# A trunk step on one core: the opening rebuilt around the first half of the tokens

## The chip, the cores and the metric

The kernel runs on one core of one Trainium2 chip, in one launch. The metric is the device time of an execution in microseconds (us); a profile beside it shows what each engine did. Engines are named as the profile names them: PE (TensorE matmuls), PEld (its weight loads), DVE (VectorE), ACT (ScalarE), POOL (GpSimd), SP (the engine that issues most DMAs).

## What is computed

One layer of a hybrid trunk over 640 tokens (512 latent, 128 context) of width 1024, in fp32. The change touches the first of its three blocks alone, the SwiGLU feed-forward with adaLN modulation:

```python
mods = (silu(cvec) @ w_ada + b_ada).reshape(9, 1024)     # one row of cvec for latent, one for context tokens
hh = rmsnorm(x, g_norm[0]) * (1 + m[1]) + m[0]
x = x + 0.5 * m[2] * ((silu(hh @ ffn1_w1) * (hh @ ffn1_w3)) @ ffn1_w2)
...
```

Behind it stand the token mixer (differential attention beside a two-way mLSTM) and a second block of this form. `ffn1_w1` and `ffn1_w3` are 1024 x 2816.

## The kernel before

Activations lie transposed: 128 partitions of features, eight pieces `d` (or `k`) of 128 features, and 640 tokens along the free axis. The tokens are cut into two halves of 320 (`HALF`); the second holds 192 latent and all 128 context tokens, which take other modulations, so a piece of it is handled in two segments of 192 and 128 (`SEGS`). A fp32 product is made of three matmuls on rounded operands (`mm3`, line 133): each operand is split into a high part (an ACT copy into `fp32r`) and a low part (DVE subtracts the high part), and high times high, high times low and low times high are added up. So every weight and every activation costs an ACT and a DVE instruction before PE can use it.

The hidden width is cut into 11 blocks of 256. Block 0 is multiplied plainly (`HalfStep.plain`, line 313) in the opening; blocks 1 to 10 go through `products` (line 406) as granules, w1 and w3 of a block in turn, with a scheme of seven products that replaces eight. That scheme needs sums and differences of the activations (`operand_sums`, line 330: a hand-ordered chain of 16 DVE instructions of 640 elements and their ACT copies) and of the weights (`Granule.parts`, line 245, which splits two pieces into wB and wC and forms sums in place in `raw`, and `Granule.sums`, line 263, which splits the 2048 columns of `raw` into ww). A granule's weights have two buffers of each kind, and `raw` has two.

The opening (lines 92 to 820) goes like this. SP loads the conditioning vectors, both halves of x, small constants, and then, in turn, eight pieces `raw_a` of 1 MB of the adaLN weights and the weights of block 0. `Modulate.__init__` squares x on ACT and adds on DVE (`Stats`, line 165), for both halves; PE adds over partitions by a matmul with ones (`ps_ss`), and ACT and DVE make the reciprocal root (`rstd_of`, line 154). `weights` splits block 0's w1 and w3 in halves; the low part of w1 is subtracted on POOL, that of w3 on DVE. Then the loop over `k`: `product(k)` is the adaLN product (16 small matmuls, `ps_a`), a DVE copy brings it to `small`, `columns(k)` turns it to columns with four tiny matmuls (`ps_at`), DVE makes `mod` and `scale`, and `norm` (line 764) makes both halves of piece k: for each segment DVE scales by scale and rstd, ACT adds the shift into the high part, DVE subtracts. After that `plain` uses piece k for three units (f, half) out of four, 18 matmuls; in each step the columns of piece k+1 and the product of k+2 stand ahead of the matmuls of k (`before`, line 772). The fourth unit, 48 matmuls, comes behind the loop. `shifts` then adds the shift to x itself on ACT, and `operand_sums` starts. The first granule's parts and sums are made as soon as their operands and an engine allow.

What sets the order: matmuls stay in the order of the program, and so do SP's transfers up to the load of `ident`. ACT, DVE and POOL are ordered by a planner of the compiler, by its own estimates and by place in the program; `issue_after(ins)` queues instructions behind `ins` on its engine.

Of the kernel before, what the change touches and what calls it, by code (L numbers as in the profile page):

```python
# [31 lines left out]
def tile_trunk(ctx: ExitStack, tc: tile.TileContext, a: dict):  # L32
# [61 lines left out]
    for hf in range(2):  # L94
        dma(x_all[:, :, hf * HALF : (hf + 1) * HALF], a["x"][:, :, hf * HALF : (hf + 1) * HALF])
    sel = load(cp, [128, 2], a["sel"], name="sel")
    b_ada = load(cp, [128, 72], a["b_ada"], name="b_ada")
    g_norm = load(cp, [128, 3, KT], a["g_norm"], name="g_norm")
# [196 lines left out]
    class HalfStep:  # L295
# [110 lines left out]
        def products(self, work, between, then=(), behind=None, prepared=False):  # L406
# [8 lines left out]
            if not prepared:  # L415
                work[0][0].parts(self.fp)
                work[0][0].sums()
# [97 lines left out]
        def run_whole(self, x, gate, final, between):  # L515
# [13 lines left out]
            self.products(work, between, down[:2])  # L529
# [163 lines left out]
    with ExitStack() as ph:  # L693
# [11 lines left out]
        class Modulate:  # L705


            def __init__(self):
                self.raw, self.row = {}, {}
                self.rs = []  # L710
                x = [x_all[:, d, :] for d in range(KT)]
                st = [Stats(x, hf, ntmp) for hf in range(2)]
                for hf in range(2):
                    for d in range(KT):
                        st[hf].add(d)
                    self.rs.append(st[hf].rstd(psum))
                self.load(0)

            def weights(self, w1, w3):

                W = [[wp.tile([128, 2048], F32R, tag="w" + t, name="wH") for t in "HL"] for _ in range(2)]
                raws = [rawp.tile([128, 2048], F32, tag="raw", name="raw") for _ in range(2)]
                for k in range(2):
                    cs = slice(1024 * k, 1024 * k + 1024)
                    for raw, src, (h, lo), eng in zip(raws, (w1, w3), W, (pool_e, vec)):
                        dma(raw[:, cs], src[:, 4 * k : 4 * k + 4])
                        act(h[:, cs], raw[:, cs], AF.Copy)
                        tt(eng, lo[:, cs], raw[:, cs], h[:, cs].bitcast(F32), ALU.subtract)
                    self.load(k + 1)
                self.load(3)  # L730
                return W
# [21 lines left out]
            def columns(self, k):  # L753
# [7 lines left out]
                for hf in range(2):  # L761
                    self.norm(hf, k)

            def norm(self, hf, d):

                c0 = hf * HALF
                S = hs.hh(d, hf)
                for s0, s1, j in SEGS[hf]:
                    xs = x_all[:, d, s0:s1]
                    h, lo = (t[:, s0 - c0 : s1 - c0] for t in S)  # L770
                    sh = m_of(0)[:, d, j : j + 1]
                    stt(xs, xs, scale[:, 0, d, j : j + 1], self.rs[hf][:, s0 - c0 : s1 - c0], ALU.mult, ALU.mult)
                    act(h, xs, AF.Identity, bias=sh)
                    stt(lo, xs, sh, h.bitcast(F32), ALU.add, ALU.subtract)

            def before(self, k):
                if k == 0:
                    self.product(0)
                    self.columns(0)
                    self.product(1)  # L780
                    self.columns(1)
                    self.product(2)
                elif k + 1 < KT:
                    self.columns(k + 1)
                    if k + 2 < KT:
                        self.product(k + 2)

            def shifts(self):
                for d in range(KT):
                    for s0, s1, j in ((0, NS, 0), (NS, T, 1)):  # L790
                        xs = x_all[:, d, s0:s1]
                        act(xs, xs, AF.Identity, bias=m_of(0)[:, d, j : j + 1])

        psum.order = [6, 7]
        start = Modulate()
        W = start.weights(a["w1a"][0], a["w3a"][0])
        units = [(0, 0), (1, 0), (0, 1)]
        psum.order = list(range(6))
        ps = {u: [acc_tile(psum) for _ in range(2)] for u in units}
# [8 lines left out]
        for u in units:  # L808
            hs.gate_plain(*u, ps[u])
        for i in range(2):  # L810
            hs.up[i].load()
        psum.order = [6, 7, 0, 1, 2, 3, 4, 5]
        ps = [acc_tile(psum) for _ in range(2)]
# [88 lines left out]
        hs.run_whole(resid, half_m[:, 0], to_mixing, modulation)  # L902
# [1101 lines left out]
```

## Time and profile before

| what | value |
|---|---|
| median of 3 runs | 1873.93 us (1870.94 to 1876.59) |
| the profiled execution | 1874.16 us |
| its span in the profile | 1872.4 us |
| PE, DVE, ACT, POOL busy | 97%, 69%, 45%, 2% of the span |
| mean granted TensorE clock | 0.988 |

Times of the trace are counted from the start of the span. Rows of the chain of waits give start, length and what ran; rows of the instructions in order of time add the engine, the line, the tiles written and read, and the count; rows of groups give count, busy time, mean length of one in ns, and idle time ahead of them. Stretches give busy time and count of PE, PEld, DVE, ACT and POOL, the granted clock as a share of full speed, the share of the DMA engines' time and GB/s. Most DVE rows carry line 39 or 42, those of the helpers `tt` and `stt`; they are told apart by their tiles.

### The profile page before, as it was taken

The page shows a single profiled execution, that of the slowest core. Times are in us where ns is not written, and L with a number is a line of the kernel's source. Part 1 is how long each engine was busy: PE and PEld are TensorE (multiplying, and loading weights), DVE is VectorE, ACT ScalarE, POOL GpSimd, SP SyncE. Part 2 cuts the span into 40 slices and gives each one's busy share as a digit, 9 for nine tenths or more (in the row PEclk, how much of TensorE's full clock was granted, in tenths as well). Part 3 has the DMA queues.
Part 4 walks back from the last instruction along what each step waited for, and adds up shares of the span by engine and source line. Part 5 has one row for each costly group of instructions (what it writes and reads, how often), then busy time and mean ns, then how long its engine had stood idle before and what let it go on. Part 6 is the DMA issues. An engine that isn't in the chain of part 4 may idle for free.

```text
span 1872.4 us, 30753 instructions
## 1 busy us (share of the span) xinstructions
PE 1812.7 (97%) x12658; PEld 1774.4 (95%) x12658; DVE 1300.2 (69%) x2177; ACT 849.6 (45%) x1455; POOL 35.8 (2%) x57
## 2 busy tenths in 40 slices
PE   5899999999999999999999989999999999999999
PEld 4899999999998999999999979999999899999999
DVE  6888886576786675865755537875456778887585
ACT  5644444112554353453454436565235645554232
POOL 1000001110000000000000000000000000000000
PEclk8899999999999999999999999999999999999999
DMA  8344547964324322322222254566442344457972
GB/s 328 119 142 168 192 169 260 382 213 146 118 81 133 123 74 95 120 77 95 98 79 83 74 178 128 187 208 218 167 134 95 130 140 153 171 177 250 336 275 91
DMA packets 127293, 299.81 MB, mean 160 GB/s; under 512 B 9457, under 2 KB 90609, under 8 KB 114353
## 3 DMA queue, kind: packets, MB, share of 16 engines
q1 hardware_dynamic: 117890, 257.49, 40.0%
q0 software_dynamic: 9264, 40.37, 5.9%
q8 instruction: 99, 1.62, 0.4%
q14 instruction: 40, 0.33, 0.0%
HBM read 234.20 MB, written 63.63 MB: 159 GB/s over the span
## 4 chain that ended last, share of the span: by engine, by line
PE 86%; DVE 7%; DMA 4%; ACT 2%; issue 1%; SPq 0%; DVEq 0%; ACTq 0%
PE ps_f L52 41%; PE ps_p L52 22%; PE ps_t L52 12%; PE ps_o L52 2%; PE sc L52 2%; PE ps_n L52 2%; PE ps_u L52 1%; DMA ada<-csil_dram 1%; PE ps_wT L55 1%; DVE ww L39 1%; PE ps_qkT L55 1%; DMA P<-nm_dram 1%; DMA so<-o_dram 0%; DVE wL L39 0%; DMA raw_a<-in_w_ada_c 0%
## 5 line engine op out<-in xcount | busy, mean ns | idle before, releaser
L52 PE MATMUL ps_f<-S,ww 128*128 128x320 f32 x1992 | 322.9, 311 | 6.7 <-ACT ww L267 4.2
L52 PEld LDWEIGHTS ps_f<-S,ww 128*128 128x128 f32 x1992 | 301.1, 189 | 9.7 <-ACT ww L267 4.5
L52 PE MATMUL ps_p<-hH,wH 128*128 128x320 f32 x864 | 274.0, 317 | 3.1 <-ACT aT L1325 2.5
L52 PE MATMUL ps_p<-hH,wL 128*128 128x320 f32 x864 | 267.3, 309 | 0.0
L52 PE MATMUL ps_p<-hL,wH 128*128 128x320 f32 x864 | 267.2, 309 | 0.0
L52 PE MATMUL ps_f<-hm,ww 128*128 128x320 f32 x1248 | 198.2, 311 | 2.0 <-DVE ww L39 2.0
L52 PEld LDWEIGHTS ps_f<-hm,ww 128*128 128x128 f32 x1248 | 188.2, 190 | 2.3 <-DVE ww L39 2.2
L52 PE MATMUL ps_t<-wH,hH 128*128 128x256 f32 x640 | 185.7, 290 | 1.0 <-DVE x L42 1.0
L52 PE MATMUL ps_t<-wH,hL 128*128 128x256 f32 x640 | 181.8, 284 | 0.0
L52 PE MATMUL ps_t<-wL,hH 128*128 128x256 f32 x640 | 181.5, 284 | 0.0
L52 PEld LDWEIGHTS ps_p<-hH,wH 128*128 128x128 f32 x864 | 162.8, 188 | 4.4 <-ACT aT L1325 2.7
L39 DVE TENSOR_TENSOR ww<-raw,ww 128x2048 fp32r<-128x2048 f32 (+1 forms) x62 | 138.7, 2237 | 37.7 <-ACT ww L267 18.7
L52 PEld LDWEIGHTS ps_p<-hL,wH 128*128 128x128 f32 x864 | 162.8, 188 | 0.5
L52 PEld LDWEIGHTS ps_p<-hH,wL 128*128 128x128 f32 x864 | 162.5, 188 | 0.0
L52 PE MATMUL ps_f<-hm,wB 128*128 128x320 f32 x1008 | 161.5, 309 | 0.0
L52 PEld LDWEIGHTS ps_f<-hm,wB 128*128 128x128 f32 x1008 | 151.3, 188 | 0.0
L39 DVE TENSOR_TENSOR wL<-raw,wH 128x2048 fp32r<-128x2048 f32 x49 | 112.1, 2289 | 38.2 <-ACT wH L123 38.1
L123 ACT ACTIVATE wH<-raw 128x2048 fp32r<-128x2048 f32 x49 | 93.6, 1911 | 89.4 <-PE ps_p L52 85.5
L39 DVE TENSOR_TENSOR raw<-raw 128x1024 f32<-128x1024 f32 x144 | 124.6, 865 | 1.9
L52 PEld LDWEIGHTS ps_t<-wH,hH 128*128 128x128 f32 x640 | 123.1, 192 | 2.0 <-issue 1.2
L52 PEld LDWEIGHTS ps_t<-wH,hL 128*128 128x128 f32 x640 | 123.1, 192 | 0.5 <-DVE hL L42 0.5
L52 PEld LDWEIGHTS ps_t<-wL,hH 128*128 128x128 f32 x640 | 123.3, 193 | 0.2
(295 smaller groups left out, 3206.0 us busy)
## 6 DMA issues: line engine op xcount, KB each, us to landing
g_dram<-g SPq DMA_DIRECT2D x44, 640.0 KB, 5.1
raw_a<-in_w_ada_c SPq DMA_DIRECT2D x24, 512.0 KB, 4.0
raw<-in_w1b SPq DMA_DIRECT2D x11, 1024.0 KB, 4.9
raw<-in_w3b SPq DMA_DIRECT2D x11, 1024.0 KB, 4.8
raw<-in_w1a SPq DMA_DIRECT2D x10, 1024.0 KB, 4.8
raw<-in_w3a SPq DMA_DIRECT2D x10, 1024.0 KB, 6.4
ada<-in_w_ada_c POOLq DMA_DIRECT2D x18, 512.0 KB, 5.3
hm<-g_dram POOLq DMA_DIRECT2D x7, 1280.0 KB, 9.6
```

Source lines behind the costliest of these rows:

```text
L39: return eng.tensor_tensor(out=out, in0=in0, in1=in1, op=op)
L52: tc.keep_in_program_order(nc.tensor.matmul(*args, **kw))
L55: tc.keep_in_program_order(nc.tensor.transpose(*args, **kw))
L123: act(h, raw, AF.Copy)
```

## The change

1. Transfers: of x only the first half is loaded at the start, in two pieces of four `d`; the second half comes behind two more `raw_a`, and block 0's weights and the small constants are moved too.
2. The first loop runs over half 0 alone: four units (two f, w1 and w3), 12 matmuls a step. The two units of half 1 for both weights, 96 matmuls, come behind it. In each step the product of k+1 stands ahead of the matmuls of k and the columns of k+1 behind them.
3. The norm: DVE multiplies whole pieces by rstd (`scaled`), ACT applies scale and shift twice, into the high part and into x (`norm`), and DVE subtracts (`low`). For half 1 (`second`), pieces 2, 3, 6 and 7 get scale and shift on DVE by tensor_scalar and one ACT copy for two pieces. `shifts` goes.
4. The second half's statistics, its rstd and the later half of block 0's weight splits move into the loop (steps 1, 3, 5 and 2), queued behind the norm of that step.
5. All subtractions of block 0's weights are DVE's.
6. The first granule's parts are queued behind the first two pieces of half 1 (`first`), the second granule's parts on DVE behind the S2 part of the operand sums (`behind`), where they had been behind the first granule's split.

```diff
     cT = load(cp, [128, KT, 2], a["cT"], name="cT")
-    for hf in range(2):
-        dma(x_all[:, :, hf * HALF : (hf + 1) * HALF], a["x"][:, :, hf * HALF : (hf + 1) * HALF])
...
+    for k in range(0, KT, 4):
+        dma(x_all[:, k : k + 4, :HALF], a["x"][:, k : k + 4, :HALF])
...
-        def products(self, work, between, then=(), behind=None, prepared=False):
+        def products(self, work, between, then=(), behind=None, prepared=False, first=()):
...
-                work[0][0].parts(self.fp)
+                with ExitStack() as st:
+                    for ins in first:
+                        st.enter_context(tc.issue_after(ins))
+                    work[0][0].parts(self.fp)
                 work[0][0].sums()
...
-            self.products(work, between, down[:2])
+            self.products(work, between, down[:2], behind=behind, first=first)
...
+                self.add(0, 0, KT)
                 self.load(0)
+                for t, n in ((sel, "sel"), (b_ada, "b_ada"), (g_norm, "g_norm")):
+                    dma(t, a[n])
+                self.raws = raws
+                self.fetch((w1, w3), 0)
+                self.load(1)
+                self.load(2)
+                dma(x_all[:, :, half(1)], a["x"][:, :, half(1)])
+                self.load(3)
+                self.fetch((w1, w3), 1)
+                self.weights(0)
+                self.rstd(0)
...
+            def weights(self, k):
+                cs = slice(1024 * k, 1024 * k + 1024)
+                for raw, (h, lo) in zip(self.raws, self.W):
+                    act(h[:, cs], raw[:, cs], AF.Copy)
+                    tt(vec, lo[:, cs], raw[:, cs], h[:, cs].bitcast(F32), ALU.subtract)
...
                 scale_of(0, 1, k, k + 1)
-                for hf in range(2):
-                    self.norm(hf, k)
+                if k == 0:
+                    self.scaled(0, 0, 1)
+                self.norm(0, k)
+                if k == 0:
+                    self.scaled(0, 1, 4)
+                self.low(0, k, 1)
+                if k == 0:
+                    self.scaled(0, 4, KT)
+
+            def scaled(self, hf, d0, d1):
+                xs = x_all[:, d0:d1, half(hf)]
+                tt(vec, xs, xs, self.rs[hf][:, None, :].to_broadcast([128, d1 - d0, HALF]), ALU.mult)
 
             def norm(self, hf, d):
...
-                    stt(xs, xs, scale[:, 0, d, j : j + 1], self.rs[hf][:, s0 - c0 : s1 - c0], ALU.mult, ALU.mult)
-                    act(h, xs, AF.Identity, bias=sh)
-                    stt(lo, xs, sh, h.bitcast(F32), ALU.add, ALU.subtract)
...
+                    by = dict(scale=scale[:, 0, d, j : j + 1], bias=m_of(0)[:, d, j : j + 1])
+                    act(h[:, s0 - c0 : s1 - c0], xs, AF.Identity, **by)
+                    self.at_act = act(xs, xs, AF.Identity, **by).ins
+
+            def low(self, hf, d, n):
+                p, k = hs.part[d // 4, hf], slice(d % 4, d % 4 + n)
+                self.at_vec = tt(vec, p[:, 1, k], x_all[:, d : d + n, half(hf)], p[:, 0, k].bitcast(F32), ALU.subtract).ins
+
+            def second(self, d):
+                if d % 4:
+                    self.norm_by_vec(d)
+                else:
+                    for i in (d, d + 1):
+                        self.norm(1, i)
+                self.low(1, d, 2)
+
+            def norm_by_vec(self, d):
+
+                for i in (d, d + 1):
+                    for s0, s1, j in SEGS[1]:
+                        xs = x_all[:, i, s0:s1]
+                        ts(xs, xs, scale[:, 0, i, j : j + 1], ALU.mult, m_of(0)[:, i, j : j + 1], ALU.add)
+                act(hs.part[d // 4, 1][:, 0, d % 4 : d % 4 + 2], x_all[:, d : d + 2, half(1)], AF.Copy)
 
-            def before(self, k):
+            def products(self, k):
+
                 if k == 0:
                     self.product(0)
                     self.columns(0)
+                elif k + 1 < KT:
+                    self.product(k + 1)
+                yield
+                if k == 0:
                     self.product(1)
...
+                if k + 1 < KT:
+                    self.columns(k + 1)
+                with tc.issue_after(self.at_act), tc.issue_after(self.at_vec):
+                    if k in (1, 3):
+                        self.add(1, 2 * k - 2, 2 * k + 2)
+                    elif k == 2:
+                        self.weights(1)
+                if k == 5:
+                    self.rstd(1)
+                    self.scaled(1, 0, 4)
+                    self.scaled(1, 4, KT)
+                elif k > 5:
+                    self.second(2 * k - 12)
...
         for k in range(KT):
-            start.before(k)
-            for u in units:
-                for i in range(2):
-                    hs.plain(ps[u][i], W[i], *u, k)
-        vec.tensor_copy(identr, ident)
+            around = start.products(k)
+            next(around)
+            for (f, i), p in ps.items():
+                hs.plain(p, W[i], f, 0, k)
+            next(around, None)
+            if k + 2 == KT:
+                first = start.at_act, start.at_vec
+        start.second(4)
+        start.second(6)
...
         for i in range(2):
-            for k in range(KT):
-                hs.plain(ps[i], W[i], 1, 1, k)
-        hs.gate_plain(1, 1, ps)
-        start.shifts()
-        hs.operand_sums(lambda r: x_all[:, 2 * r : 2 * r + 2, :])
+            for f in range(2):
+                for k in range(KT):
+                    hs.plain(ps[f, i], W[i], f, 1, k)
+        for f in range(2):
+            hs.gate_plain(f, 1, (ps[f, 0], ps[f, 1]))
+        summed = hs.operand_sums(lambda r: x_all[:, 2 * r : 2 * r + 2, :])
```

More of the change, by code (lines that the diff above doesn't have):

```diff
@@ L513, in up_work, with run_whole @@
             ]
-        def run_whole(self, x, gate, final, between):
+        def run_whole(self, x, gate, final, between, behind, first):
             work = self.up_work()
@@ L719, in weights @@
[L719 to L729, printed above, removed]
-                self.load(3)
-                return W
+                self.st = [Stats(x, hf, ntmp) for hf in range(2)]
@@ new lines, in __init__, with add, rstd, fetch @@
+                dma(x_all[:, :, half(1)], a["x"][:, :, half(1)])
+                self.load(3)
+                self.fetch((w1, w3), 1)
+                self.weights(0)
+                self.rstd(0)
+            def add(self, hf, d0, d1):
+                for d in range(d0, d1):
+                    self.st[hf].add(d)
+            def rstd(self, hf):
+                self.rs[hf] = self.st[hf].rstd(psum)
+            def fetch(self, srcs, k):
+                for raw, src in zip(self.raws, srcs):
+                    dma(raw[:, 1024 * k : 1024 * k + 1024], src[:, 4 * k : 4 * k + 4])
@@ L800, in tile_trunk @@
+                if k == 5:
[4 more added lines that the diff above has]
+                    self.second(2 * k - 12)
+        psum.order = [6, 7]
+        start = Modulate(a["w1a"][0], a["w3a"][0])
+        W = start.W
+        psum.order = list(range(4))
+        ps = {(f, i): acc_tile(psum) for f in range(2) for i in range(2)}
         psum.order = [6, 7]
         for k in range(KT):
-            start.before(k)
```

49 lines of the change are left out of this document (15 added, 34 removed).

## The prediction

> **What bounds the kernel now.** I read the page first, then the stretches of 20 us, then the chain of waits, then the instructions in order of time from 0 to 90 us. The page says that TensorE (PE) is busy for 97% of the span, so there is little to win anywhere; the stretches say that the little is in the first 100 us.
>
> ```profile
> span 1872.4 us, 30753 instructions
> PE 1812.7 (97%) x12658; PEld 1774.4 (95%) x12658; DVE 1300.2 (69%) x2177; ACT 849.6 (45%) x1455; POOL 35.8 (2%) x57
> ```
>
> In the stretches the columns are PE, weight load, DVE, ACT, POOL, then the granted clock and the DMA. PE is full from 100 us on. Before that it lacks time in the first 30 us and in 80 to 100, and DVE is nearly full from 40 to 80.
>
> ```profile
> 20.00:40.00 20.00, 15.04 (x120) 11.44 (x116) 15.43 (x37) 9.37 (x19) 2.65 (x2) 0.74 1.02 419
> 40.00:60.00 20.00, 20.00 (x174) 17.78 (x167) 18.19 (x49) 14.76 (x30) 0.00 (x0) 1.00 0.07 27
> 60.00:80.00 20.00, 19.77 (x132) 19.05 (x130) 18.60 (x24) 13.37 (x21) 0.00 (x0) 1.00 0.25 86
> 80.00:100.00 20.00, 14.36 (x76) 13.91 (x76) 13.59 (x15) 9.55 (x11) 1.25 (x2) 0.74 0.64 224
> 100.00:120.00 20.00, 20.00 (x138) 20.00 (x137) 15.50 (x21) 8.69 (x14) 0.53 (x1) 1.00 0.49 164
> ```
>
> The chain (start, length, what) names the two places. The first loop starts at 30.3 behind the load of x, the norm and the first adaLN columns; each later turn is PE alone, 2.83 + 0.34 + 1.00 = 4.17 us. At 81.7 DVE ends the sums on the raw weights of the second granule, ACT and DVE split them in turn, and from 86.60 PE runs on for 394 matmuls. I call 86.60 the mark: behind it the work is the same in both kernels and PE is full, so the change is worth what it moves the mark.
>
> ```profile
> 1.20 6.79 DMA x<-in_x
> ...
> 12.41 2.52 PE ps_ss L52 x4
> ...
> 30.30 4.76 PE ps_f L52 x18
> ...
> 36.40 2.83 PE ps_f L52 x18
> 39.23 0.34 PE ps_at L52 x4
> 39.58 1.00 PE ps_a L52 x16
> ...
> 81.68 0.61 DVE raw L39
> 82.31 1.92 ACT ww L267
> 84.25 2.30 DVE ww L39
> ...
> 86.60 60.73 PE ps_f L52 x394
> ```
>
> **The start, up to the first matmuls.** Three things shorten it. Only half of x is needed, in two pieces: the first lands between 4.6 (half of 6.79, from 1.20) and 7.99; I take 6.2. The adds run without a gap at 0.58 us each, the first 0.88 us behind the landing; six then end at 10.6 and not at 12.36. The second half's statistics leave the start. And the GpSimd subtraction goes, which stretches DVE instructions beside it: in the same newton step one instruction takes 0.49 us and the next, under POOL's, 2.65. Twice that is 4.3 us saved.
>
> ```profile
> 8.87 3.48 DVE L39 TENSOR_TENSOR nacc<-nacc,nsq 128x320 f32<-128x320 f32 x6 [7.59 <-ACT nsq L181]
> ...
> 17.26 0.49 DVE L39 TENSOR_TENSOR rt<-rt,rv 128x320 f32<-128x320 f32 x1
> ...
> 17.73 2.35 POOL L39 TENSOR_TENSOR wH<-raw,wH 128x1024 fp32r<-128x1024 f32 x1 [17.28 <-ACT wH L727]
> 17.78 2.65 DVE L42 SCALAR_TENSOR_TENSOR ry<-rt,ry 128x320 f32<-128x320 f32 x1
> ```
>
> New start: 10.6, ps_ss 2.5, then rstd in six instructions of about 0.5 (3.1 with hand-overs) = 16.2. The two weight splits that now are both DVE's (1.2 us each, the wB row below) stand ahead of it; 1.5 us of them is not covered by ps_ss: 17.7. Then the first scaled piece 0.5, ACT's two pieces 1.05, the subtraction 0.5, and the two larger scaled pieces, which come first in the program and of which 1.2 us isn't covered by ACT: 21.0. So the loop starts fed at 21 (19 to 23) and not at 30.3.
>
> **The first loop.** A turn holds 12 matmuls for 18, so 1.89 + 0.34 + 1.00 = 3.2 us of PE. But the columns of step k+1 now stand behind the matmuls of step k, and between them and their own matmuls PE has only one product (1.00 us). In that time must pass: mod and scale 0.16 each, ACT's h and x (0.56 each, overlapping by 0.09), the subtraction 0.49, and five hand-overs of 0.04.
>
> ```profile
> L39 DVE TENSOR_TENSOR mod<-ps_at,b_ada 128x4 f32<-128x4 f32 x8 | 1.3, 158 | 4.8 <-PE ps_at L52 4.8
> L773 ACT ACTIVATE hm<-x,mod 128x320 fp32r<-128x320 f32 x8 | 4.5, 563 | 12.3 <-DVE x L42 12.2
> L746 DVE COPY small<-ps_a 128x256 f32<-128x256 f32 x8 | 3.3, 416 | 0.0
> L39 DVE TENSOR_TENSOR s<-ps_f,u 128x320 f32<-128x320 f32 x1 | 0.5, 486 | 0.0
> ```
>
> That is 2.04 us against 1.00, less one matmul that needs h alone: PE, which keeps program order and so holds all that is behind, waits 0.9 us a turn, and the turn is 4.1 us, nearly that of before for two thirds of the work. Before, the columns stood a whole step ahead and this chain was hidden. This is the step I hold to be the weak one. From 21: step 0 at half clock (12/18 of 4.76 = 3.2), product 1.0, its copy and columns 0.9, the chain 2.0 = 28.1; six turns = 52.7. What the change queues in the loop adds to it: rstd of the second half (four ps_ss on PE, 2.5 us at the start's slow pace, some 1.4 here, 0.5 beyond the wait), two weight splits on DVE (0.7 of their 2.4 reach the chain), and the scaled pieces of the second half (1280 elements each, by the g row's 1.49 us for as many), which stand ahead of mod 7 on DVE or behind it: 0 to 2.8, I take 1.8. The last step's matmuls start at 55.7 (53 to 58). DMA does not set this: before, it moved 419 GB/s in 20 to 40 us and was all but done then (27 GB/s in 40 to 60), and the loop is over no earlier here. The next granules' loads now wait for the second weight splits, near 40 us, and land about 5 us later, ahead of their use.
>
> ```profile
> raw<-in_w1a SPq DMA_DIRECT2D x10, 1024.0 KB, 4.8
> ```
>
> ```profile
> 56.19 12.56 PE L52 MATMUL ps_f<-hm,wH 128*128 128x320 f32 x84
> ```
>
> PE then has 12 + 96 matmuls, at this row's 0.15 each 16.1 us: it is done at 71.8 at the earliest, as the 96 may wait for the second half's pieces. Before, this row ended the same work at 68.7. PE is 3 us late there, but that isn't yet the mark.
>
> **DVE behind the loop.** From 61.3 to 82.3 DVE had no gap of note: these are most of its rows there (count, busy, mean ns), and the stretch is 21.0 us.
>
> ```profile
> L39 DVE TENSOR_TENSOR x<-x 128x640 f32<-128x640 f32 x7 | 5.6, 819 | 0.0
> L39 DVE TENSOR_TENSOR S<-x,S 128x640 fp32r<-128x640 f32 x6 | 4.7, 818 | 0.0
> L39 DVE TENSOR_TENSOR ww<-raw,ww 128x2048 fp32r<-128x2048 f32 x1 | 2.3, 2286 | 0.0
> L39 DVE TENSOR_TENSOR g<-SO,g 128x1280 fp32r<-128x1280 f32 x1 | 1.5, 1486 | 0.0
> L39 DVE TENSOR_TENSOR raw<-raw 128x512 f32<-128x512 f32 x2 | 1.4, 686 | 0.0
> L39 DVE TENSOR_TENSOR raw<-raw 128x1024 f32<-128x1024 f32 x1 | 1.2, 1222 | 0.0
> L39 DVE TENSOR_TENSOR wB<-raw,wB 128x1024 fp32r<-128x1024 f32 x1 | 1.2, 1218 | 0.0
> L39 DVE TENSOR_TENSOR wC<-raw,wC 128x512 fp32r<-128x512 f32 x1 | 0.7, 684 | 0.0
> ```
>
> All of it stays. What the loop did before now falls behind it: the first granule's parts (wB, wC and three raw: 4.1 us without overlaps), which the change holds back until the second half has begun; four subtractions of 640 (0.73 each when queued, 2.9); one operand sum (0.7); and eight tensor_scalar of 192 and 128. For these no row stands: above, 0.41 and 0.35 us of the fused form of the same sizes; below, 0.15; 1.2 to 3.0 in all, I take 2.0.
>
> ```profile
> L42 DVE SCALAR_TENSOR_TENSOR x<-x,scale,ry 128x192 f32<-128x192 f32 x8 | 3.3, 411 | 0.0
> L42 DVE SCALAR_TENSOR_TENSOR x<-x,scale,ry 128x128 f32<-128x128 f32 x8 | 2.8, 345 | 0.0
> ```
>
> By the Trainium skill (VectorE: DVE Perf Modes, the perf-mode tier table) an fp32 tensor_scalar in SBUF runs at twice the rate of a two-tensor form, which by its figure of 1227 ns for 2048 makes some 1.4 of these 2.0, and the mark 0.6 earlier; no row here shows it.
>
> So 21.0 + 4.1 + 2.9 + 0.7 + 2.0 = 30.7 us from 55.7, plus some 0.8 in which DVE waits for ACT, which has 18 pieces of the second half to do: 87.2 where it was 82.3, 5 us late. ACT's and DVE's last split follow as before. Dearer may be the order.
>
> ```profile
> 70.04 1.22 DVE L39 TENSOR_TENSOR wB<-raw,wB 128x1024 fp32r<-128x1024 f32 x1
> ```
>
> The first granule's parts come after the operand sums in the program. If they are done after them, its five products wait too, and up to 60 matmuls (8.9 us) are left when the second granule's weights are ready; if they are slotted in early, nothing. I take 3, nearer to early, since the row shows the second granule's wB done at 70.0, amid the sums. The mark moves by 5 + 3 = 8 us. The half clock behind the stall stays, as the stall does.
>
> **Sum.** The profiled execution took 1874.16 us around its span of 1872.4, 0.2 above the median of 1873.93. With 8 us: 1882.
>
> **Rivals.** *Faster:* the chain is hidden, turns are PE's own 3.2 us. Last step at 46.6, DVE's 30.7 end at 77.3, the mark at 81.5; with pieces of the second half done in the loop's gaps 78.5, so 1866. It decides for turns under 3.5 us. For it speaks that DVE has work for only some 23 of the loop's 35 us (1.25 a step, adds 3.5, splits 2.4, rstd 2, scaled pieces 5.4); against it, the chain, each link of which waits for the one before. *Even:* the last step at 53, the first granule's parts early: 53 + 30.7 = 83.7 for 82.3, no surcharge: 1874 to 1878. *Half clock in the loop:* PE idles a fifth of each turn. Before, it was halved behind the stall (first row, 0.50); but a stretch as thin as this loop kept it whole (second row, 1.00).
>
> ```profile
> 82.30:92.60 10.30, 6.90 (x24) 6.51 (x25) 6.55 (x6) 3.82 (x2) 0.54 (x1) 0.50 0.87 308
> 713.80:717.20 3.40, 1.92 (x15) 1.61 (x14) 3.40 (x6) 0.60 (x1) 0.00 (x0) 1.00 0.29 77
> ```
>
> If it comes, 12 matmuls cost 1.3 us more in seven turns, 9 us: 1891. The Trainium skill (TensorE: Matmul & The Clock Gate, "A second HAM failure mode: psum-queue depth-cycling") says that short idles between groups of matmuls make the clock swing; the row at 713.80 speaks against it here. *It doesn't do what it says:* a planner orders ACT and DVE, and puts splits or statistics ahead of the first norm, so that the loop starts no earlier than 27: 6 us more, 1888.
>
> **Chances.** Forecast 0.44 (its own range 1877 to 1888), even 0.20, faster 0.21, half clock 0.08, late start 0.07. A measurement of this kernel tells 0.3%, 5.6 us, from no change. Faster by more: most of its case, 0.19. Within: the even case, the lower end of the forecast and the rest, 0.26. Slower: 0.55. The range reaches down to the faster case's 1866, of which half may fall below, and up to the half clock's 1891.
>
> **What would show it.** Right: first loop matmuls near 21; turns of 4.1 with PE waiting for the subtraction of x; the last step near 55.7; DVE without gaps from there to about 87; the split of the second granule's ww behind 90. Wrong: turns of 3.2; a loop over before 50; or the first granule's parts done inside the loop. If PE never stops from the loop into the second granule, the forecast is wrong as a whole.

## The result, and the profile after

The changed kernel takes 1882.27 us (median of 4 runs, 1881.32 to 1883.22), the kernel before, run beside it, 1872.43 us: a ratio of 1.0049, 95% interval 1.0033 to 1.0065. It is slower, and 1882 was forecast. The number came out, in good part by luck: two of the steps that make it up did not come out, and one of those decides what one would repair. The profiled execution took 1883.22 us around a span of 1881.5. One execution of f2, a kernel of the experiments below, took 8873 us and is left out of its ratio.

The stretches of 20 us after, from 40 us on (columns as before: PE, weight load, DVE, ACT, POOL, granted clock, DMA):

```profile
40.00:60.00 20.00, 15.34 (x132) 11.38 (x124) 12.12 (x27) 9.85 (x17) 0.00 (x0) 1.00 0.32 121
60.00:80.00 20.00, 7.78 (x38) 7.43 (x39) 18.09 (x33) 17.32 (x33) 0.00 (x0) 0.66 0.00 0
80.00:100.00 20.00, 20.00 (x139) 20.00 (x138) 18.16 (x21) 12.42 (x15) 1.21 (x2) 1.00 0.50 157
```

Before, PE lacked 5.6 us in 80 to 100 and was full from 40 to 80. Now it is full from 80 on, but has a quarter of its time idle in 40 to 60 and 12 us in 60 to 80, where ACT and DVE are nearly full.

From 120 us on both kernels do the same work, so the simplest measure of the opening is how many matmuls PE has begun by then. One row for each kernel, before first (PE's busy time, count):

```profile
0.00:120.00 120.00, 95.18 (x643) 0.91 0.56 207
```

```profile
0.00:120.00 120.00, 83.36 (x563) 0.89 0.50 183
```

That is 80 matmuls fewer. At the pace of a full stretch (138 in 20 us, the kernel before from 100 to 120: 0.145 us each) the opening lost 11.6 us; the busy times say the same, 11.8 us. I use this count below. It is that of one execution, and good to some 2 us: three of the kernels below are the same up to the loop and start it at 25.87, 26.87 and 27.14.

Where PE stands still shows in its instructions in order of time around the last step of the first loop (start, length, count, and in brackets the idle time before and what ended it):

```profile
47.21 1.88 PE L52 MATMUL ps_f<-hm,wH 128*128 128x320 f32 x11 [0.80 <-DVE hm L39]
...
51.77 1.88 PE L52 MATMUL ps_f<-hm,wH 128*128 128x320 f32 x11 [0.80 <-DVE hm L39]
...
58.06 0.50 PE L52 MATMUL ps_at<-sel,small 128*128 128x2 f32 x4
69.50 0.64 PE L52 MATMUL ps_f<-hm,wH 128*128 128x320 f32 x1 [10.94 <-ACT hm L798]
72.85 3.57 PE L52 MATMUL ps_f<-hm,wH 128*128 128x320 f32 x12 [2.72 <-DVE hm L39]
```

The columns of the last piece are there at 58.06, yet its matmuls wait for ACT until 69.50 and for DVE until 72.85. From there PE runs on without a stop. DVE's and ACT's instructions in that time show what stood ahead:

```profile
58.33 2.89 DVE L39 TENSOR_TENSOR x<-x,ry 128x1280 f32<-128x1280 f32 x2
61.14 0.15 DVE L39 TENSOR_TENSOR mod<-ps_at,b_ada 128x4 f32<-128x4 f32 x1
61.21 1.72 DVE L48 TENSOR_SCALAR x<-x,scale,mod 128x192 f32<-128x192 f32 x6
62.84 0.15 DVE L42 SCALAR_TENSOR_TENSOR scale<-mod,g_norm 128x2 f32<-128x2 f32 x1
```

```profile
59.85 1.75 ACT L798 ACTIVATE hm<-x,mod,scale 128x192 fp32r<-128x192 f32 x4 [3.14 <-DVE x L39]
...
66.27 1.04 ACT L252 ACTIVATE wB<-raw 128x1024 fp32r<-128x1024 f32 x1
...
68.80 0.64 ACT L798 ACTIVATE hm<-x,mod,scale 128x320 fp32r<-128x320 f32 x1
```

The second half's scaled pieces stand ahead of the last piece's `mod`, six tensor_scalar of the second half ahead of its `scale`, and the second half's pieces and the copies of both granules' weights ahead of its norm on ACT.

### The profile page after: what moved, and what is told of

Its sections match the earlier page's. It is cut to its first block, busy times and chain, and to the rows that moved or that the text cites. A ratio compares the mean times of both kernels' runs of the same rounds, so it can differ in the third digit from the quotient of the medians.

```text
span 1881.5 us, 30716 instructions
## 1 busy us (share of the span) xinstructions
PE 1813.2 (96%) x12658; PEld 1774.0 (94%) x12658; DVE 1296.6 (69%) x2156; ACT 848.9 (45%) x1449; POOL 30.9 (2%) x55
## 4 chain that ended last, share of the span: by engine, by line
PE 83%; DVE 8%; DMA 4%; ACT 3%; issue 1%; SPq 0%; DVEq 0%; ACTq 0%
PE ps_f L52 38%; PE ps_p L52 22%; PE ps_t L52 12%; PE sc L52 2%; PE ps_o L52 2%; PE ps_n L52 2%; DMA ada<-csil_dram 2%; DVE ww L39 1%; PE ps_wT L55 1%; PE ps_qkT L55 1%; PE ps_u L52 1%; DMA raw<-in_w2b 1%; DVE x L39 1%; DVE hm L39 0%; DMA raw_a<-in_w_ada_c 0%
```

## The experiments

Four theories. **C**: the chain in each turn, the step that the prediction held to be the weak one. **Q**: the queue just shown, the last piece behind second-half work. **H**: behind a loop over one half, PE has nothing to do until the other half's pieces are there. **D**: VectorE's list behind the loop sets the end, as the prediction reckoned the mark. No kernel below leaves out or changes what is computed. Each ratio is to executions of the kernel before that were taken beside it, with medians of 1871.6 to 1872.5 us. The count is that of the profiled execution alone, which took 1869.8 us in e3 (median 1874.58) and 1878.47 in f2 (median 1871.1): count and median need not agree.

| kernel | us, median | ratio to before, 95% interval | matmuls by 120 us | opening against before |
|---|---|---|---|---|
| before | 1872.4 | | 643 | |
| changed | 1882.27 | 1.0049 (1.0033 to 1.0065) | 563 | -11.6 us |
| e1 last piece first | 1885.8 | 1.0069 (1.0052 to 1.0087) | 565 | -11.3 |
| e2 second half early | 1890.44 | 1.0102 (1.0087 to 1.0117) | 535 | -15.7 |
| e3 columns ahead | 1874.58 | 1.0008 (0.9999 to 1.0018) | 656 | +1.9 |
| e4 both | 1874.89 | 1.0015 (1.0004 to 1.0027) | 634 | -1.3 |
| e5 GpSimd back | 1892.82 | 1.0093 (1.0073 to 1.0112) | 538 | -15.2 |
| e6 columns ahead, start | 1873.83 | 1.0001 (0.9989 to 1.0013) | 653 | +1.5 |
| e7 both, splits early | 1875.28 | 1.0016 (1.0006 to 1.0027) | 612 | -4.5 |
| b1 before, no GpSimd | 1868.13 | 0.9972 (0.9961 to 0.9984) | 688 | +6.5 |
| f1 b1, granule first | 1867.66 | 0.9977 (0.9967 to 0.9987) | 676 | +4.8 |
| f2 f1, x in pieces | 1871.1 | 1.0000 (0.9988 to 1.0011) | 671 | +4.1 |
| f3 f1, csil behind | 1865.38 | 0.9962 (0.9949 to 0.9975) | 700 | +8.3 |

**e1, the last piece first (Q against H).**

```diff
                 if k == 5:
                     self.rstd(1)
-                    self.scaled(1, 0, 4)
-                    self.scaled(1, 4, KT)
                 elif k > 5:
-                    self.second(2 * k - 12)
+                    with tc.issue_after(self.at_act), tc.issue_after(self.at_vec):
+                        if k == 6:
+                            self.scaled(1, 0, 4)
+                            self.scaled(1, 4, KT)
+                        self.second(2 * k - 12)
```

> Only the order around the last piece of the first half changes: its columns, norm and subtraction go ahead of the second half's scaled pieces and norm on ACT and DVE. Theory Q (the queue: the 11.0 and 2.7 us that TensorE waits ahead of the last loop step are there because that piece's norm stands behind second-half work) expects the last step near 61 and some 11 to 13 us back, 1870. Theory H (the half: behind the loop over the first half TensorE has nothing to do until the second half's pieces are there, and these start only with their rstd at 58.3) expects the last step near 61 too, but the same wait then in front of the second half's matmuls, until about 72, and 0 to 3 us back: 1879 to 1882.

PE in order of time:

```profile
60.53 2.28 PE L52 MATMUL ps_f<-hm,wH 128*128 128x320 f32 x11 [0.80 <-DVE hm L39]
63.35 0.63 PE L52 MATMUL ps_f<-hm,wH 128*128 128x320 f32 x1 [0.54 <-ACT hm L798]
68.32 1.70 PE L52 MATMUL ps_f<-hm,wH 128*128 128x320 f32 x5 [4.34 <-DVE hm L39]
73.29 0.64 PE L52 MATMUL ps_f<-hm,wH 128*128 128x320 f32 x1 [3.27 <-ACT hm L819]
75.23 4.97 PE L52 MATMUL ps_f<-hm,wH 128*128 128x320 f32 x21 [1.30 <-DVE hm L39]
```

The last step runs at 60.53, 12.3 us earlier, and nothing comes of it: the wait is now in front of the second half's matmuls, 0.54 + 4.34 + 3.27 + 1.30 = 9.45 us. Most of the other 2.9 us go in a longer stretch at a granted clock of 0.50, from 61.8 to 78.9, with 7.64 us of PE's work in it. The time lies above what either theory expected. Q falls as a cause: it names the place of the stop in the changed kernel, not what makes PE wait.

**e2, the second half early (H).**

```diff
-                    if k in (1, 3):
-                        self.add(1, 2 * k - 2, 2 * k + 2)
+                    if k < 2:
+                        self.add(1, 4 * k, 4 * k + 4)
                     elif k == 2:
                         self.weights(1)
-                if k == 5:
-                    self.rstd(1)
-                    self.scaled(1, 0, 4)
-                    self.scaled(1, 4, KT)
-                elif k > 5:
-                    self.second(2 * k - 12)
+                    elif k == 3:
+                        self.rstd(1)
+                    elif k < 7:
+                        self.scaled(1, 2 * k - 8, 2 * k - 6)
+                        self.second(2 * k - 8)
...
-        start.second(4)
+        start.scaled(1, 6, 8)
         start.second(6)
```

> The second half's squares are summed in turns 0 and 1 and not in 1 and 3, its rstd comes in turn 3 and not 5, and its pieces are scaled and normed by pairs in turns 4 to 6. Theory H expects no wait of over 2 us between the loop and the first granule, the plain part done near 76 (90.3 in the changed kernel), and 9 to 14 us back: 1868 to 1873. Theory Q expects about the same, since nothing large stands ahead of the last piece any more. Theory C (the chain of each turn, the recorded forecast's weak step) expects turns of 4.6 or longer by what is put into them, up to 5.2, and at most 6 us back: 1876 or more. Theory D (DVE's list behind the loop sets the end) expects the second granule's weight split to end no earlier than 30 us behind the loop less the 9 us that moved into it, near 80, and a new stop of TensorE there.

```profile
58.14 2.83 PE L52 MATMUL ps_f<-hm,wH 128*128 128x320 f32 x11 [1.23 <-DVE hm L39]
...
64.91 5.60 PE L52 MATMUL ps_f<-hm,wH 128*128 128x320 f32 x24 [1.51 <-DVE hm L39]
...
90.04 4.76 PE L52 MATMUL ps_f<-S,ww 128*128 128x320 f32 x22 [4.75 <-DVE ww L39]
...
99.79 3.51 PE L52 MATMUL ps_f<-S,ww 128*128 128x320 f32 x12 [3.23 <-ACT u L403]
```

```profile
96.98 0.63 ACT L252 ACTIVATE wC<-raw 128x512 fp32r<-128x512 f32 x1 [7.89 <-DMA raw<-in_w1a]
```

A miss for H, and for Q. The wait behind the loop does go (1.51 us and less), and the plain part is done at 83 and not at 90.3. But the last turn takes 6.8 us (58.14 to 64.91), as what was put into the loop lies in its chain, and PE then stops at the first granule's `ww` until 90.04 and once more at that granule's last product, until 99.79. What it needs there is a copy on ACT (`u`), which stood behind two weight copies, the first of them waiting 7.89 us for a load. The count is 28 matmuls below the changed kernel's. C predicted the longer turn and D a stop behind the loop, though at the second granule.

**e3, the columns ahead again (C).**

```diff
                 if k == 0:
                     self.product(0)
                     self.columns(0)
-                elif k + 1 < KT:
-                    self.product(k + 1)
-                yield
-                if k == 0:
                     self.product(1)
                 if k + 1 < KT:
                     self.columns(k + 1)
+                if k + 2 < KT:
+                    self.product(k + 2)
+                yield
```

> Undoes one part of the change: columns of step k+1 and the product of step k+2 stand ahead of the matmuls of step k again, as in the kernel before; all else as changed. Theory C expects turns of 3.2 to 3.5 us, and all that follows earlier by 6 to 8 us: 1874 to 1876. Theory H expects the same shift of the second half's rstd, to about 51, and a wait in front of the second half's matmuls that stays near 11 us: 1874 to 1876. Theory Q expects the last piece's norm to be done a turn ahead, so that its wait goes as well: 1864 to 1868.

```profile
38.15 2.02 PE L52 MATMUL ps_f<-hm,wH 128*128 128x320 f32 x12
...
41.44 2.03 PE L52 MATMUL ps_f<-hm,wH 128*128 128x320 f32 x12
...
47.62 1.88 PE L52 MATMUL ps_f<-hm,wH 128*128 128x320 f32 x11 [0.71 <-DVE hm L39]
51.04 0.41 PE L52 MATMUL ps_f<-hm,wH 128*128 128x320 f32 x1 [1.54 <-ACT hm L798]
56.01 1.70 PE L52 MATMUL ps_f<-hm,wH 128*128 128x320 f32 x5 [4.57 <-DVE hm L39]
59.15 0.64 PE L52 MATMUL ps_f<-hm,wH 128*128 128x320 f32 x1 [1.44 <-ACT hm L819]
60.56 1.97 PE L52 MATMUL ps_f<-hm,wH 128*128 128x320 f32 x6 [0.77 <-DVE hm L39]
```

A turn is now 3.29 us (38.15 to 41.44), PE's own time, against 4.56. The last step runs at 47.62 and not at 72.85, and nothing behind the loop had to be changed for that. 7.7 us come back in the medians, 13.5 in the count, 11.4 of them by the seventh step (44.75 for 56.11). Undoing this one part brings the time back to that of the kernel before (1.0008, 0.9999 to 1.0018). Behind the loop PE still waits 1.54 + 4.57 + 1.44 + 0.77 = 8.3 us for the second half's pieces, as H says.

**e4, both.** The diffs of e2 and e3 together.

> The two edits before together: columns ahead, and the second half's statistics and pieces inside the loop. If C and H each hold a part of the loss, both come back: turns of 3.3 to 3.8, no stop behind the loop, 1858 to 1866. If DVE's list is the next bound (D), TensorE stops at the second granule's weights as in the kernel before, and the time is within 2 us of the run with the second half early alone.

The wait for the second half shrinks, and PE stops at the first granule instead:

```profile
49.60 6.93 PE L52 MATMUL ps_f<-hm,wH 128*128 128x320 f32 x29 [2.41 <-DVE hm L39]
...
78.73 5.04 PE L52 MATMUL ps_f<-S,ww 128*128 128x320 f32 x22 [5.17 <-DVE ww L39]
```

DVE is busy for 20.00 of the 20 us from 60 to 80 and comes to the first granule's `ww` at 76.39. With the chain out of the way D is the next bound, at the first granule and not at the second, where D had it: the time is e3's. Both expected times are missed, 1858 to 1866 and that of e2.

**e7, both, with the splits early (D).** On e4, the first granule's parts are no longer held back, and its `ww` is split ahead of the operand sums that follow S1's.

```diff
-            self.products(work, between, down[:2], behind=behind, first=first)
+            self.products(work, between, down[:2], behind=behind, prepared=True)
...
+        hs.up[0].parts(fp)
+        hs.up[0].sums()
-        summed = hs.operand_sums(lambda r: x_all[:, 2 * r : 2 * r + 2, :])
+        summed = hs.operand_sums(lambda r: x_all[:, 2 * r : 2 * r + 2, :], hs.up[0].split_ins)
...
+                if split is not None and (f, i, r) == (low, S1, 1):
+                    prev = split
```

> On the run with columns ahead and the second half early: the first granule's parts are no longer held back, and its weights are split ahead of the later operand sums on VectorE. Theory D (what stops TensorE there is that VectorE is full from 59.7 and comes to that split at 76.5) expects the split near 68, the stop of 5.2 us at 78.7 gone or under 1.5, and 4 to 6 us back: 1868 to 1871. If the loop loses what is put into it, or the stop goes to the next operand, the time stays at 1874 to 1876.

```profile
51.61 7.23 PE L52 MATMUL ps_f<-hm,wH 128*128 128x320 f32 x36 [4.89 <-DVE hm L39]
61.81 13.98 PE L52 MATMUL ps_f<-hm,wH 128*128 128x320 f32 x83 [2.98 <-DVE hm L39]
...
89.54 0.90 PE L52 MATMUL ps_f<-S,ww 128*128 128x320 f32 x2 [3.18 <-ACT ww L267]
```

The stop of 5.2 us goes, and 7.9 us of waits stand in front of the second half again, with another 4.6 at the second granule (3.18, and 1.43 at 91.86). Moving a piece of DVE's list forward made the next piece late here, and the time stays. That the sum of the list counts, as D has it, and not the place of one split, fits this but isn't shown by it.

**b1, the kernel before without GpSimd's arithmetic.**

```diff
-                    for raw, src, (h, lo), eng in zip(raws, (w1, w3), W, (pool_e, vec)):
+                    for raw, src, (h, lo), eng in zip(raws, (w1, w3), W, (vec, vec)):
```

> The kernel before with one part of the change: VectorE and not GpSimd subtracts the first matrix's halves. The recorded forecast's term (GpSimd's subtraction stretches two DVE instructions of the norm by 2.2 us each) expects the norm's step of 0.5 us to stay 0.5, the first loop to be fed 2 to 4 us before 30.3, as 1.2 us of split stand on DVE for it, and 1869 to 1871. The rival (the opening of the kernel before waits for its transfers, not for DVE) expects the loop at 30 and no change of the time.

DVE's newton step in b1, and PE's first loop step:

```profile
18.89 0.48 DVE L42 SCALAR_TENSOR_TENSOR ry<-rt,ry 128x320 f32<-128x320 f32 x1
```

```profile
25.87 2.91 PE L52 MATMUL ps_f<-hm,wH 128*128 128x320 f32 x18
...
78.80 0.90 PE L52 MATMUL ps_f<-S,ww 128*128 128x320 f32 x2 [4.21 <-ACT ww L267]
81.12 3.04 PE L52 MATMUL ps_f<-S,ww 128*128 128x320 f32 x10 [1.43 <-DVE ww L39]
```

The step that took 2.65 us takes 0.48, the loop starts 4.4 us earlier (30.30 before), and its first step runs at the full clock in this execution (2.91 us for 4.76). One word of the kernel before, and it is faster by 0.28% (0.16 to 0.39).

**e5, the changed kernel with GpSimd's subtractions back.** The same word, the other way.

> The changed kernel with GpSimd's subtractions of the first matrix put back. The recorded forecast's term expects a stretched instruction in the norm again, the loop fed at 25 to 27 and not at 23.0, and the time up by 2 to 4 us, 1884 to 1886. If the start is no bound any more, since TensorE waits 13.7 us further on, the last step's place stays within 1 us of 72.85 and the time within 2 us of 1882.

The loop is fed only 0.7 us later (23.74 for 23.02). Dearer is the second pair of weight splits, inside the loop: GpSimd takes 2.38 us from 43.54, DVE's subtraction beside it 2.56 for 1.22, and the next step waits for that:

```profile
43.54 2.38 POOL L39 TENSOR_TENSOR wH<-raw,wH 128x1024 fp32r<-128x1024 f32 x1 [27.63 <-ACT wH L747]
44.45 2.56 DVE L39 TENSOR_TENSOR wH<-raw,wH 128x1024 fp32r<-128x1024 f32 x1 [1.40 <-ACT wH L747]
```

In the count 25 matmuls, 3.6 us; in the medians 10.5. Neither expectation holds: the loop was to be fed at 25 to 27, or the time to stay. The 7 us between the two lie behind 120 us, where nothing was changed. In the profiled executions some 6 of them arise near 1130 and 1513 us, where e5 has stretches at a granted clock of 0.50 (6.8 us from 1131.7, 3.4 from 1510.6) and the changed kernel none at the same place of the program. Why they fall there stays open.

**e6, the start.** On e3: the seven larger pieces of the first half are scaled behind the first piece's norm, and the third product stands behind the first step.

```diff
                 self.norm(0, k)
-                if k == 0:
-                    self.scaled(0, 1, 4)
                 self.low(0, k, 1)
                 if k == 0:
-                    self.scaled(0, 4, KT)
+                    with tc.issue_after(self.at_vec):
+                        self.scaled(0, 1, 4)
+                        self.scaled(0, 4, KT)
```

> On the run with the columns ahead: the seven scaled pieces of the first half go behind the first piece's norm on VectorE (2.5 us stood ahead of it), and the third product, whose weights land at 22, behind the first step's matmuls. If the start is worth what it looks like, the first step is fed near 20.5 and all behind it comes 2 us or more earlier, 1871 to 1873. Theory H (behind the loop TensorE waits for the second half's pieces) expects the wait of some 8 us behind the loop to stay; theory D (VectorE's list sets the end) expects 0 to 1 us of it at the second granule.

The first step is fed at 21.23 and not at 24.16, but takes 3.55 us at half clock; the next begins at 28.72 and not at 27.99, as the third product is now in between. Nothing is gained, by count or time: a miss. The wait behind the loop stays (1.55 + 4.56 + 1.44 + 0.77), as H expected.

**f1, f2, f3: what stops b1.** In b1 PE stops 5.6 us at the second granule. f1 puts that granule's sums and its split ahead of S4's operand sums and of the gated block's split on DVE; f2 adds the x pieces of the change's transfer order; f3 puts ACT's Silu of the conditioning rows behind the third granule's split.

```diff
+        def mid():
+            g0, g1 = hs.up[:2]
+            g0.parts(fp)
+            g0.sums()
+            with tc.issue_after(g0.split_at):
+                g1.parts(fp)
+            g1.sums()
+            return g1.summed
-        hs.operand_sums(lambda r: x_all[:, 2 * r : 2 * r + 2, :])
+        hs.operand_sums(lambda r: x_all[:, 2 * r : 2 * r + 2, :], mid)
...
-        hs.store_g(hs.SO, 0)
+        with tc.issue_after(hs.low_at):
+            hs.store_g(hs.SO, 0)
...
+                if mid is not None and (f, i, r) == (terms, S4, 0):
+                    prev = mid()
```

In f3:

```diff
-        act(csil, csil, AF.Silu)
...
+            if (i, at) == (1, 1):
+                with tc.issue_after(hs.up[2].copied):
+                    act(csil, csil, AF.Silu)
```

> On the kernel before without GpSimd's arithmetic: the second granule's sums on the raw weights and its split are put ahead of the last two operand sums and of the split of the gated block on VectorE. Theory D (in the kernel before the order of VectorE's list behind the loop alone sets the end of the opening) expects the split to end near 76.5 and not at 81, TensorE's stop before the second granule down from 5.6 us to 2 or less, the last operand's halves ready as they are needed, and 3 to 5 us back: 1863 to 1865. If the stop only passes on to the last operand, which is now late by as much, the time stays at 1868.

> The same, and of the change's order of transfers only the two pieces of the first half of x, ahead of the second half in one. If the start waits for the first landing of x, as the recorded forecast's start has it, the squares begin 2 to 2.5 us earlier and the loop is fed at 23.5 to 24.5 and not at 25.9: 1861 to 1864. If it waits for the adaLN weights of the third product, which land near 22 to 25 in both, the loop starts within 0.5 us of the run before, and the time is the same.

> The run with the second granule first gave its 5 us back at the third granule: ScalarE's piece on the loaded conditioning rows (1.9 us, landing at 88.2) stood ahead of the split of that granule's weights, whose sums were done at 84.9, and TensorE stopped there for 4.1 us, from 89.65 on. Here that piece goes behind the split. If that was the cause, ScalarE copies the weights near 85, the stop goes, and 5 to 7 us come back in the opening: 1860 to 1863. If the next thing on VectorE's list is late in its place, the stop stays and the time is that of the run before, 1867 to 1868.

f1, PE and then ACT:

```profile
77.36 1.73 PE L52 MATMUL ps_f<-S,ww 128*128 128x320 f32 x10 [1.76 <-DVE ww L39]
...
92.00 0.56 PE L52 MATMUL ps_f<-S,ww 128*128 128x320 f32 x2 [2.35 <-ACT ww L267]
94.33 3.03 PE L52 MATMUL ps_f<-S,ww 128*128 128x320 f32 x10 [1.77 <-DVE ww L39]
```

```profile
88.24 1.91 ACT L843 ACTIVATE csil<-csil 128x2048 f32<-128x2048 f32 x1 [5.15 <-DMA csil<-in_c_rows]
90.06 1.89 ACT L267 ACTIVATE ww<-raw 128x2048 fp32r<-128x2048 f32 x1
```

The stop shrinks from 5.6 to 1.76 us as expected, and 4.1 us are given back one granule later: ACT had waited 5.15 us for a transfer, with a copy queued behind that was ready. In f3 this stop is gone and the second granule's stays at 1.77. f3 has the lowest ratio, 0.9962 of before, and the count is 57 matmuls ahead; 1860 to 1863 us were expected. Its interval overlaps with those of f1 and b1, so its lead on them rests on the count of single executions (24 and 12 matmuls). f2 is a miss: the squares of x begin at 5.56 and not at f1's 7.91, yet the loop is fed at 28.44, later than f1's 26.87, so the first landing of x is no bound of this start.

## Why the prediction was right, and where not

**The size: met in good part by luck.** The mark was to move by 8 us. It moved by 14.2, from 86.60 to this row:

```profile
100.83 1.92 PE L52 MATMUL ps_f<-S,ww 128*128 128x320 f32 x12
```

Right behind it 2.5 us come back, as the stretch at 0.50 that the prediction shows there, to 92.6, is gone: the products with `wC` that follow begin at 106.11 for 94.36, 11.75 later, and the count says 11.6. Another 2.5 come back behind the opening (last section), and the profiled executions end 9.1 apart. The forecast had the work behind the mark unchanged. Its 8 us agree with the end because the far too late last step, a surcharge that wasn't paid and these 5 us all but cancel.

**The start: right, 2 us late.** Fed at 21 (19 to 23) was forecast, 23.0 measured. The 1.2 us taken for the two larger scaled pieces were 2.5: `mod` is done at 18.5, `scale` comes at 20.92. GpSimd's term, 4.3 us, is 3.2 to 4.4 at the loop in b1, f1 and f3 (25.87 to 27.14 for 30.30). In the changed kernel its removal saves 0.7 at the start, and more inside the loop (e5).

**The turn: the mechanism right, mis-sized.** 4.1 us forecast, 4.56 measured (47.21 to 51.77), PE waiting for the subtraction of x as said. The term that was off is ACT's two pieces, taken from the form with a bias alone, 563 ns and overlapping. With scale and bias both read from columns they take 650 each, one behind the other (`h` here, `x` likewise 652):

```profile
L798 ACT ACTIVATE hm<-x,mod,scale 128x320 fp32r<-128x320 f32 x8 | 5.2, 651 | 25.3 <-DVE scale L42 25.3
```

The Trainium skill (ScalarE: Activation LUTs, "What ACT_TABLE_LOAD costs") adds some 93 ns for each operand that is a pointer, an estimate of 640 ns by its figures for this form; the rows agree (651). The overlap of 93 ns that it gives for two in a row doesn't show between these two: the second starts 0.69 us behind the first (45.98 and 45.29).

The first turn took 8.67 us (23.02 to 31.69) for 7.1 forecast, and the second, under the half clock, 5.97.

That this is the weak step is shown: e3 undoes it alone and the loss is gone. The rival with turns of 3.2 us is what e3 built; it ran at 1874.6 and not at the rival's 1866, with 8.3 us of waits behind the loop.

**The last step: here the prediction failed.** It put "the scaled pieces of the second half ... ahead of mod 7 on DVE or behind it: 0 to 2.8, I take 1.8", and the last step at 55.7 (53 to 58). The planner put the second half's norm and both granules' copies ahead too: 69.50 and 72.85. Against e1, where they stand behind and the step runs at 60.53, that is 12.3 us for the 1.8. Behind it stood "done at 71.8 at the earliest, as the 96 may wait for the second half's pieces", a wait named and not priced. e1 measures it, 9.45 us, e3 again, 8.3. Had I set the second half's rstd (58.3) and ACT's 18 pieces behind it against PE's need, it would have been the first stop, ahead of the mark's.

**DVE's list: the sum right, in part by luck.** It ends, with its waits, in these rows:

```profile
92.03 1.40 DVE L39 TENSOR_TENSOR raw<-raw 128x512 f32<-128x512 f32 x2
93.86 1.49 DVE L39 TENSOR_TENSOR g<-SO,g 128x1280 fp32r<-128x1280 f32 x1 [0.42 <-ACT g L381]
96.18 2.29 DVE L39 TENSOR_TENSOR ww<-raw,ww 128x2048 fp32r<-128x2048 f32 x1 [0.82 <-ACT ww L267]
```

From 58.33 to the end of the second granule's raw sums at 93.4 are 35.1 us; without the two scaled pieces (2.9) and the last piece's mod, scale and subtraction (some 0.8) that is 31.4, for 30.7 and 0.8 of waits forecast. But the 21.0 us that were to stay held the split of `g` (1.5) and a sum `s` (0.5), and both now come behind the raw sums, `s` at 100.56. In their place stand waits, 2.2 us (DVE is busy for 32.94 of the 35.10) for 0.8, and tensor_scalar: the six shown above take 1.72 us and the other two 0.64, 2.4 for 2.0. From the Trainium skill's page VectorE: DVE Perf Modes (the perf-mode tier table) the prediction took an estimate of 1.4, which pieces of 192 and 128 columns don't reach. In proportion to the 1227 ns that it quotes for 2048 elements, the 1280 of all eight would be an estimate of 0.8, so the 1.4 doesn't follow as it stands. Since the loop ended later than 55.7, the end is 93.4 and not 87.2.

**The order: wrong.** 3 us were added for the first granule's parts coming late. DVE did them at 65.9 to 71.6, ahead of the operand sums: nothing. As PE's last step came at 72.85, that was also inside the loop, which the prediction had named as a sign of being wrong.

**The mark and "what would show it".** The split of the second granule's `ww` stands behind 90, at 96.18, as said. But PE came to it only at 100.83, with the weights ready. PE did not stop from 72.85 into the second granule, and for that case the prediction had said that "the forecast is wrong as a whole". The end that it forecast, DVE's list, does fail as the cause: it was 2.4 us from being the bound (the split ends at 98.47). e4 and e7 show that it is next in line.

**The half clock.** "Stays, as the stall does": 10.3 us at 0.50 before, from 82.3; after, they follow the new stall:

```profile
32.10:35.50 3.40, 3.40 (x19) 3.33 (x21) 0.15 (x1) 0.00 (x0) 0.00 (x0) 0.50 0.89 347
62.80:76.50 13.70, 4.28 (x15) 3.94 (x16) 11.79 (x20) 11.79 (x22) 0.00 (x0) 0.50 0.00 0
```

PE worked only 4.28 us of the second, so it cost an estimated 2. In the loop the clock fell for one stretch of 3.4 us; from 40 to 60, with PE idle for a quarter of the time, it was 1.00. The rival of a half clock in the loop holds for one turn in seven.

**Left open.** Between e3 (656) and b1 (688) lie 4.6 us: a loop over one half with its wait for the other, the new norm and the order of transfers, which were not taken apart further. f2 says that the pieces of x alone gain nothing.

## What to carry to other kernels

Shortening a loop body moves work out of its cover: before adding up what is saved, set the chain that each turn must wait for against what PE has left to do beside it, and look for what PE does between the loop and the moment at which the work pushed behind it is ready. When a stop is removed, follow the list of the engine that ended it: e1, e7 and f1 each gave the time back one wait later. The stop that f3 took out, and one in e2, came from an engine waiting for a transfer ahead of work that was ready. Undo parts one by one, in both directions: one word of this change alone was faster than either kernel.

## What the runs showed of the hardware

Three things I had not expected. GpSimd's subtraction stretches DVE's two-tensor subtraction beside it as it does the fused form: 2.56 us for 1.22 (e5). The first step of the loop, the same instructions up to there in b1, f1 and f3, took 2.91, 3.44 and 4.86 us, at full, mixed and half clock; the Trainium skill (TensorE: Matmul & The Clock Gate, "The HAM clock gate") says that the window of 3.4 us by which the clock is set runs freely, so that the same kernel has more or fewer slow matmuls from run to run, and this agrees. And a part of the opening's loss was taken up a millisecond later. The same 127 matmuls, at the same place of the program, in the kernel before and in the changed one:

```profile
1096.60:1127.70 31.10, 22.42 (x127) 20.36 (x126) 10.48 (x24) 15.28 (x39) 0.00 (x0) 0.89 0.66 208
```

```profile
1109.20:1136.80 27.60, 21.39 (x127) 20.07 (x127) 10.60 (x26) 13.79 (x36) 0.00 (x0) 0.94 0.75 235
```

They take 3.5 us less in the changed kernel. 1.0 of that is PE's own time, at a mean granted clock of 0.94 for 0.89. The rest is idle time, most of it one wait, 6.21 us before and 3.74 after, for a piece that DVE makes from a load (`P<-nm_dram`):

```profile
1118.10 1.20 PE L52 MATMUL ps_n<-va,P 128*128 128x258 f32 x2 [6.21 <-DVE P L39]
```

There the changed kernel makes up at least part of the 2.5 us between the opening's 11.6 and the executions' 9.1. Why the clock falls where it does isn't settled; differences of 2 to 4 us between kernels in single executions should not be read as effects of an edit.
